# A hybrid attention and RWKV-7 block: each attention step's small matmuls tied into one group, low-rank products issued ahead of both sigmoids, the last chunk's outputs tied together

## The chip, the cores and the metric

One core of one Trainium2 chip runs the whole kernel. The metric is the device time in microseconds (us) of one execution; a run is repeated and its median taken. Lower is better.

## What is computed

One decoder layer on x of 256 x 1024 float32. After an RMS norm, one wide projection feeds two causal token mixers side by side, attention (8 heads of 64, one block of 256, so it is plain causal attention with a linear distance bias) and an RWKV-7 recurrence (8 heads of 64). Each mixer's output is gated by a SiLU path, projected up, multiplied by a sigmoid gate, and the sum goes through one output projection and a second norm.

```
h = rmsnorm(x, norm_pre);  proj = h @ w_in
aq, ak, av, az, rw_stream, rz, g_att, g_rw = split(proj)
ya = attention(aq, ak, av) * silu(az)
rs, ksr, vs, wd, ad = token_shift_mix(rw_stream)
decay = exp(-exp(-softplus(-(w0 + tanh(wd) @ w_up)) - 0.5))     # low-rank product 1
a     = sigmoid(a0 + ad @ a_up)                                 # low-rank product 2
o  = rwkv7_scan(rs, decay, kmod(ksr, a), vs, kk(ksr), a)
yb = (head_groupnorm(o) + bonus) * silu(rz)
u  = sigmoid(g_att) * (ya @ w_up_att) + sigmoid(g_rw) * (yb @ w_up_rw)
out = x + rmsnorm(u @ w_out, norm_post)
```

## The kernel before, in words

**The stream.** All projections run on TensorE in blocks of 512 KB of weights. A block arrives by DMA (tile wraw, issued on SyncE's queue, L117), is split into a rounded high part on ScalarE (whi, L123) and a remainder on VectorE (wlo, L124), and is then used by `proj_tile` (L259) or `up_pair` (L697) through `mm3` (L136): three matmuls of 128 x 128 weights on 256 columns (L137, L138, L139) for each eighth of the block, 24 in all. Splits run up to LOOKAHEAD = 4 blocks ahead. These 24 matmuls a block are the main stream. Their results lie in one of three large PSUM tiles (mmps).

**The lanes.** Everything else on TensorE is small and is let into the stream by hand. Two generators, one for the recurrence (`rw`) and one for attention (`att`), give up control at each `yield`. `pump()` is called three times in a block (after its 3rd, 5th and 8th eighth, L267); each call adds the lane's rate to its credit, and at a credit of 1 the generator runs to its next `yield`. So a rate of 0.32 is one piece of attention for every 3.1 pumps, about one a block. This sets the program's order. A list scheduler then orders each engine's instructions at compile time by that order and by its own model of when operands are ready; a stream matmul that it takes to be unready leaves a hole that a later small matmul may fill. On the chip each engine runs its instructions in the order so fixed, and waits on semaphores.

**Ties.** `one_group` (L334) adds an ordering edge, without a semaphore, from the first matmul of a list to each of the others: none of them can stand ahead of the first. `after` (L329) is that edge; it also keeps sigmoids behind the last softmax (`last_soft`) and exponentials behind the low-rank sigmoids (`last_sig`), for ScalarE's function tables.

**The low-rank products** (`lora_phase`, L339). For each of four head pairs, a small PSUM tile (smps, three of them in all) holds both products. Two matmuls (L347) make the first, a sigmoid on ScalarE (L348) reads it, two more matmuls make the second in the same bank, and a second sigmoid reads that.

**Attention** (`att_phase`, L665) has six steps p = 0 to 5, one for each head pair and two to empty the pipeline. In a step come, each behind a `yield`: the values of pair p - 2 (`att_values`, 4 matmuls written, 8 issued, L658, 128 rows by 64 columns of the array), the transposes of pair p - 1 (`att_transpose`, 6, L651, the full array), and the scores of pair p with its softmax (`att_scores`, 4 written, 8 issued, L628, 64 rows by 128 columns, into the one tile twops). The softmax is VectorE (L635, L637, L642) and ScalarE (L640 to L644); the transposes read it, and ScalarE copies them to pt (L653) for the values, whose result it copies to att_o (L663).

**The recurrence** runs pair phases (`pair_phase`, L372), a triangular inverse of 31 steps on VectorE (`inverse_phase`, L447; L477, L479), then four chunks one after another (`chunks_phase`, L545). In each chunk, L551 makes u, VectorE scales it to UVE and UVO (L554), L561 gives the next state, L523 the next chunk's input, and `chunk_out` (L529; L536 from the state, L538 from UVE and UVO) the output. For chunks 0 to 2 the outputs are tied in one group behind the next chunk's input; the last chunk's outputs stand untied:

```
            if c == NCH - 1:
                chunk_out(c)
```

Each output is then normalised over VectorE and GpSimd (`norm_chunk`, L574) and transposed (L586) for the up-projection of the recurrence, which is the last to use `up_pair`. The output projection (L844) and a short tail on VectorE and the DMA queues end the kernel.

Of the kernel before, what the change touches and what calls it, by code (L numbers as in the profile page):

```python
# [16 lines left out]
P = 128  # L17
T = 256
# [11 lines left out]
WARM = 26  # L30
HP = 100000
HP_FROM = 5
R_ATT, R_SUB, R_CH = 0.32, 0.75, 0.8
NORM_SLOTS = 4
LORA_SLOTS = 4
LOOKAHEAD = 4
# [7 lines left out]
def block_kernel(ctx: ExitStack, tc: tile.TileContext, x, wp, pv, lora, npost, out):  # L44
# [294 lines left out]
    def lora_phase():  # L339
        for _ in range(LORA_SLOTS):  # L340
            yield
        for p in range(NP):
            pl = smps().rearrange("p (n t) -> p n t", n=2)
            fs = slice(p * P, (p + 1) * P)
            for n, (dst, off, lst) in enumerate(((sga, PV_W0, sgs), (aaa, PV_A0, aas))):
                for i in range(2):
                    nc.tensor.matmul(out=pl[:, n], lhsT=lrs[:, n, fs], rhs=wax[:, i, n], start=(i == 0), stop=(i == 1))  # L347
                last_sig.append(nc.scalar.activation(out=dst[:, p, :], in_=pl[:, n], func=AF.Sigmoid, bias=pvc(off, p)))  # L348
                lst.append(dst[:, p, :])
            yield  # L350
# [175 lines left out]
        nc.scalar.copy(out=wsb, in_=w)  # L526
        return wsb, mms

    def chunk_out(c):  # L529


        o = p4(smps())
        mms = []
        for p in range(NP):
            for h, fs, AR, SV, UV, SC in (EV, OD):
                mms.append(mm(out=o[fs, p, :], lhsT=AR[:, p, c, C:2 * C], rhs=SV[:, c, p, :], start=True, stop=False))  # L536
            for h, fs, AR, SV, UV, SC in (EV, OD):
                mms.append(mm(out=o[fs, p, :], lhsT=SC[:, p, c, C:2 * C], rhs=UV[:, c, p, :], start=False, stop=True))  # L538
        o2, osb = p4(tg()), p4(tg())
        nc.scalar.activation(out=o2, in_=o, func=AF.Square)  # L540
        nc.scalar.copy(out=osb, in_=o)
        nm.gens.append(norm_chunk(c, osb, o2))
        return mms

    def chunks_phase():  # L545
# [3 lines left out]
        for c in range(NCH):  # L549
            u = p4(smps())  # L550
            one_group([mm(out=u[fs, p, :], lhsT=X64[fs, p, c, :], rhs=wsb[fs, p, :], start=True, stop=True)  # L551
                       for p in range(NP) for h, fs, AR, SV, UV, SC in (EV, OD)])
            for h, fs, AR, SV, UV, SC in (EV, OD):
                nc.vector.tensor_tensor(out=UV[fs, c], in0=u[fs], in1=rnt[fs, :, c:c + 1].broadcast_to([64, NP, C]), op=ALU.mult)  # L554
            yield
            if c == NCH - 1:
                chunk_out(c)
                yield
                break
            s = p4(smps())  # L560
            one_group([mm(out=s[fs, p, :], lhsT=BKt[:, c, h, p, :], rhs=UV[:, c, p, :], start=True, stop=True)  # L561
                       for p in range(NP) for h, fs, AR, SV, UV, SC in (OD, EV)])
            for h, fs, AR, SV, UV, SC in (EV, OD):
                gc = Gc[fs, :, c, :].broadcast_to([64, NP, C])
                dst = SV[fs, c + 1]
                nc.vector.tensor_tensor(out=dst, in0=s[fs], in1=SV[fs, c], op=ALU.add)
                nc.vector.tensor_tensor(out=dst, in0=dst, in1=gc, op=ALU.mult)
            yield

            wsb, mms = chunk_in(c + 1)  # L570
            one_group(mms + chunk_out(c))
            yield
# [51 lines left out]
    def att_scores(p):  # L624

        qT, kT = qk
        s = twops()
        one_group([nc.tensor.matmul(out=s[:, i, c0:c0 + n], lhsT=qT[LH[i], p, q0:q0 + P], rhs=kT[LH[i], p, 0:n], start=True, stop=True)  # L628
                   for q0, n, c0 in ((0, P, 0), (P, T, P)) for i in (1, 0)])
        for i in range(2):  # L630
            h = 2 * p + i
            lg = tt([P, 384], "lg")
# [12 lines left out]
            lgs[h] = lg  # L645

    def att_transpose(p):
        for h in (2 * p, 2 * p + 1):
            tp = smps()
            for b in range(3):  # L650
                nc.tensor.transpose(out=tp[:, b * P:(b + 1) * P], in_=lgs[h][:, b * P:(b + 1) * P], identity=ident)  # L651
            pts[h] = tt([P, 384], "pt")
            nc.scalar.copy(out=pts[h], in_=tp[:, 0:384])  # L653

    def att_values(p):

        o = smps()
        one_group([nc.tensor.matmul(out=o[LH[i], t0:T], lhsT=vtk[:, b, p * P + i * 64:p * P + i * 64 + 64], rhs=pts[2 * p + i][:, c0:c0 + T - t0],  # L658
                                    start=(b == 0), stop=(b == 1)) for b, t0, c0 in ((0, 0, 0), (1, P, T)) for i in (1, 0)])
        if p == 0:  # L660
            att_all.append(ct([P, NP, T], "gz"))
        att_o[p] = att_all[0][:, p, :]
        nc.scalar.copy(out=att_o[p], in_=o[:, 0:T])  # L663

    def att_phase():  # L665

        for p in range(NP + 2):
            if 2 <= p:
                att_values(p - 2)
            yield  # L670
            if 1 <= p <= NP:
                att_transpose(p - 1)
            yield
            if p < NP:
                att_scores(p)
            yield

    def silu(ps, sg):
# [75 lines left out]
    def main():  # L754
# [16 lines left out]
        for p in range(NP):  # L771
# [5 lines left out]
            with hp():  # L777
                nc.scalar.copy(out=kT[:, p, :], in_=ps)
            if p == 0:
                att.rate = R_ATT  # L780
                att.gens.append(att_phase())
            yield

# [160 lines left out]
```

## Time and profile before

| | |
|---|---|
| median of 3 runs | 256.84 us (256.5 to 257.18) |
| profiled execution, its own time | 255.78 us |
| its span (first to last instruction) | 254.1 us |
| TensorE matmul busy | 240.2 us, 95% of the span |
| VectorE busy | 181.6 us, 71% |
| ScalarE busy | 148.9 us, 59% |
| GpSimd busy | 32.8 us, 13% |
| mean granted TensorE clock | 0.987 of full |

The span is the profiled execution's; what lies around it in its own time of 255.78 us is 1.7 us of start and end. Busy time is the union of an engine's instructions; matmuls overlap, so the distance from the start of one to the start of the next says what it costs in the stream, and its own duration does not. Lines such as L347 are those of the kernel before.

### The profile page before, as it was taken

How to read it: one execution, taken by the hardware profiler on the slowest of the kernel's cores; microseconds unless marked ns; L12 is line 12 of the kernel's file. 1: busy time of each engine (PE TensorE's matmuls, PEld its weight loads, DVE VectorE, ACT ScalarE, POOL GpSimd, SP SyncE). 2: the span in 40 equal slices, each digit the busy share in tenths (PEclk: the TensorE clock that was granted, in tenths of full speed). 3: DMA queues.
4: the chain of work that ended last, by engine and by line, in shares of the span. 5: the costliest groups of instructions: out<-in, count | busy, mean ns of one | idle time of the engine just before them, and what ended most of it. 6: DMA issues, size and time to landing. Idle time of an engine off the chain costs nothing.

```text
span 254.1 us, 5784 instructions
## 1 busy us (share of the span) xinstructions
PE 240.2 (95%) x2283; PEld 220.2 (87%) x2283; DVE 181.6 (71%) x370; ACT 148.9 (59%) x291; POOL 32.8 (13%) x74
## 2 busy tenths in 40 slices
PE   7799699999999999999999999999998999999990
PEld 5599699998788999899898999899896999988890
DVE  2677739999853089999996366987777666998243
ACT  4676799577517277693949765763333543573241
POOL 2735000103015200000004400000112100000000
PEclk9979999999999999999999999999999999999997
DMA  6825955865769958534345576434225766543022
GB/s 232 350 81 152 357 178 181 250 172 134 187 158 216 294 172 277 168 126 144 146 168 146 163 237 201 147 93 161 84 83 181 238 194 215 172 143 106 3 72 94
DMA packets 19500, 43.68 MB, mean 172 GB/s; under 512 B 7536, under 2 KB 8688, under 8 KB 19472
## 3 DMA queue, kind: packets, MB, share of 16 engines
q1 hardware_dynamic: 18336, 41.30, 51.6%
q0 software_dynamic: 704, 1.71, 2.7%
q8 instruction: 18, 0.29, 0.5%
q10 hardware_dynamic: 432, 0.29, 0.4%
q14 instruction: 10, 0.08, 0.1%
HBM read 37.90 MB, written 1.84 MB: 156 GB/s over the span
## 4 chain that ended last, share of the span: by engine, by line
PE 61%; DVE 16%; ACT 8%; DMA 7%; issue 5%; POOL 1%; DVEq 0%; SPq 0%; ACTq 0%; POOLq 0%
PE mmps L137 14%; PE mmps L139 13%; PE mmps L138 13%; PE mmps L844 9%; DVE wlo L124 5%; ACT whi L123 4%; DMA wraw<-in_wp_dram 3%; DVE gen L477 2%; PE mmps L612 2%; DMA BK<-BK 2%; DMA slot<-in_x_dram 2%; DVE slot L479 2%; ACT hh L184 1%; PE smps L347 1%; DVE hl L185 1%
## 5 line engine op out<-in xcount | busy, mean ns | idle before, releaser
L137 PE MATMUL mmps<-hh,whi 128*128 128x256 f32 x336 | 96.7, 288 | 0.0
L138 PE MATMUL mmps<-hl,whi 128*128 128x256 f32 x336 | 94.9, 282 | 0.0
L139 PE MATMUL mmps<-hh,wlo 128*128 128x256 f32 x336 | 94.8, 282 | 0.0
L124 DVE TENSOR_TENSOR wlo<-wraw,whi 128x1024 fp32r<-128x1024 f32 x58 | 71.4, 1234 | 28.2 <-ACT whi L123 27.9
L123 ACT CAST whi<-wraw 128x1024 fp32r<-128x1024 f32 x58 | 60.5, 1048 | 36.8 <-PE mmps L138 21.9
L137 PEld LDWEIGHTS mmps<-hh,whi 128*128 128x128 f32 x336 | 63.3, 188 | 2.7 <-issue 2.0
L139 PEld LDWEIGHTS mmps<-hh,wlo 128*128 128x128 f32 x336 | 63.2, 188 | 0.4
L138 PEld LDWEIGHTS mmps<-hl,whi 128*128 128x128 f32 x336 | 63.3, 188 | 0.3
L477 DVE SCALAR_TENSOR_TENSOR gen<-slot,rnf 64x31 f32<-64x31 f32 (+15 forms) x31 | 12.1, 392 | 0.7
L479 DVE TENSOR_TENSOR slot<-slot,gen 64x31 f32<-64x31 f32 (+15 forms) x31 | 10.3, 333 | 0.7
L580 POOL TENSOR_TENSOR rv<-rv,mhalf 128x4 f32<-128x4 f32 x4 | 4.2, 1049 | 44.7 <-DVE rv L579 44.7
L137 PE MATMUL mmps<-yah,whi 128*128 128x256 f32 x32 | 9.2, 287 | 0.0
L850 DVE TENSOR_TENSOR SCE<-mmps,X 128x512 f32<-128x512 f32 (+1 forms) x5 | 2.9, 583 | 8.7 <-ACT ar L849 8.7
L139 PE MATMUL mmps<-slot,wlo 128*128 128x256 f32 x32 | 9.1, 283 | 0.0
L137 PE MATMUL mmps<-slot,whi 128*128 128x256 f32 x32 | 9.1, 283 | 0.0
L138 PE MATMUL mmps<-slot,whi 128*128 128x256 f32 x32 | 9.1, 283 | 0.0
L138 PE MATMUL mmps<-yal,whi 128*128 128x256 f32 x32 | 9.0, 281 | 0.0
L139 PE MATMUL mmps<-yah,wlo 128*128 128x256 f32 x32 | 9.0, 281 | 0.0
L849 ACT ACTIVATE ar<-mmps 128x512 f32<-128x512 f32 (+1 forms) x5 | 2.6, 513 | 10.7 <-PE mmps L844 10.7
L640 ACT ACTIVATE lg<-lg,mn 128x128 f32<-128x128 f32 x8 | 3.2, 397 | 8.3 <-DVE mn L635 8.3
L191 PE MATMUL mmps<-hl,whi 128*128 128x256 f32 x24 | 7.5, 336 | 0.5 <-DVE hl L185 0.2
L190 PE MATMUL mmps<-hh,whi 128*128 128x256 f32 x24 | 7.6, 339 | 0.2
(260 smaller groups left out, 502.3 us busy)
## 6 DMA issues: line engine op xcount, KB each, us to landing
wraw<-in_wp_dram SPq DMA_DIRECT2D x64, 512.0 KB, 4.2
slot<-in_x_dram SPq DMA_DIRECT2D x2, 512.0 KB, 4.0
wraw<-in_wp_dram SPq DMA_DIRECT2D x2, 256.0 KB, 5.3
gz<-in_lora_dram SPq DMA_DIRECT2D x1, 512.0 KB, 8.1
bonv<-gen SPq DMA_DIRECT2D x8, 64.0 KB, 3.1
ARE<-ar SPq DMA_DIRECT2D x4, 128.0 KB, 3.1
ARO<-ar SPq DMA_DIRECT2D x4, 128.0 KB, 3.1
ARE<-SCE SPq DMA_DIRECT2D x4, 128.0 KB, 2.5
```

Of the source, the lines that this page charges most:

```text
L123: cast = nc.scalar.copy(out=hi[:, a:b], in_=raw[:, a:b])
L124: nc.vector.tensor_tensor(out=lo[:, a:b], in0=raw[:, a:b], in1=hi[:, a:b], op=ALU.subtract)
L137: nc.tensor.matmul(out=o, lhsT=lh, rhs=rh, start=first, stop=False)
L138: nc.tensor.matmul(out=o, lhsT=lh, rhs=rl, start=False, stop=False)
L139: nc.tensor.matmul(out=o, lhsT=ll, rhs=rh, start=False, stop=last)
L190: nc.tensor.matmul(out=started[n][:, 0:T], lhsT=ws, rhs=hh[:, k, :], start=(k == 0), stop=False)
L191: nc.tensor.matmul(out=started[n][:, 0:T], lhsT=ws, rhs=hl[:, k, :], start=False, stop=False)
L477: nc.vector.scalar_tensor_tensor(out=pr, in0=fl[:, s, s + 1:32].unsqueeze(2).broadcast_to([64, n, s + 1]), scalar=rnf[:, s:s + 1], in1=tb[ ...
L479: nc.vector.tensor_tensor(out=tb[:, s + 1:32, 0:s + 1], in0=tb[:, s + 1:32, 0:s + 1], in1=pr, op=ALU.add)
L580: nc.gpsimd.tensor_tensor(out=rv, in0=rv, in1=mhalf, op=ALU.pow)
L612: nc.tensor.matmul(out=pa[i], lhsT=a[:, k, ts], rhs=w[:, wsl], start=(k == 0 and n == 0), stop=(k == KD - 1 and n == 2))
L844: nc.tensor.matmul(out=ps, lhsT=a[:, k, ts], rhs=w[:, wsl], start=(k == 0 and m == 0), stop=(k == KD - 1 and m == 2))
```

## The change

In `lora_phase` all four matmuls of a pair are issued before its two sigmoids. In `att_phase` a step's three pieces are issued at one pump in place of three, in the order values, scores, transposes, and tied to the first matmul among them; the softmax follows. The lane's rate falls to a third (0.32 to 0.107), and it starts with a credit of 0.7, so its steps fall on pumps 3, 13, 22, 31, 41 and 50 after the first key block. Before, the scores fell on pumps 10, 19, 29 and 38, the transposes on 16, 25, 35 and 44, the values on 22, 32, 41 and 50. In `att_transpose` both PSUM tiles are taken and written before either is copied. `chunk_out` for the last chunk is tied in one group and multiplies with UVO and UVE first, then with the state. The diff, cut where lines only move:

```diff
-R_ATT, R_SUB, R_CH = 0.32, 0.75, 0.8
+R_ATT, R_SUB, R_CH = 0.107, 0.75, 0.8
...
 def lora_phase():
...
-            for n, (dst, off, lst) in enumerate(((sga, PV_W0, sgs), (aaa, PV_A0, aas))):
+            for n in range(2):
                 for i in range(2):
                     nc.tensor.matmul(out=pl[:, n], lhsT=lrs[:, n, fs], rhs=wax[:, i, n], start=(i == 0), stop=(i == 1))
+            for n, (dst, off, lst) in enumerate(((sga, PV_W0, sgs), (aaa, PV_A0, aas))):
                 last_sig.append(nc.scalar.activation(out=dst[:, p, :], in_=pl[:, n], func=AF.Sigmoid, bias=pvc(off, p)))
                 lst.append(dst[:, p, :])
...
-    def chunk_out(c):
+    def chunk_out(c, late=True):
...
         for p in range(NP):
-            for h, fs, AR, SV, UV, SC in (EV, OD):
-                mms.append(mm(out=o[fs, p, :], lhsT=AR[:, p, c, C:2 * C], rhs=SV[:, c, p, :], start=True, stop=False))
-            for h, fs, AR, SV, UV, SC in (EV, OD):
-                mms.append(mm(out=o[fs, p, :], lhsT=SC[:, p, c, C:2 * C], rhs=UV[:, c, p, :], start=False, stop=True))
+            for n in range(2):
+                for h, fs, AR, SV, UV, SC in (EV, OD) if late else (OD, EV):
+                    a, b = ((AR, SV), (SC, UV))[n ^ (not late)]
+                    mms.append(mm(out=o[fs, p, :], lhsT=a[:, p, c, C:2 * C], rhs=b[:, c, p, :], start=(n == 0), stop=(n == 1)))
...
             if c == NCH - 1:
-                chunk_out(c)
+                one_group(chunk_out(c, late=False))
...
     def att_scores(p):
...
-        one_group([nc.tensor.matmul(out=s[:, i, c0:c0 + n], ...) ...])
+        return s, [nc.tensor.matmul(out=s[:, i, c0:c0 + n], ...) ...]
+
+    def att_softmax(p, s):
         for i in range(2):
...
     def att_transpose(p):
-        for h in (2 * p, 2 * p + 1):
-            tp = smps()
+        tps, mms = [smps(), smps()], []
+        for i, tp in enumerate(tps):
             for b in range(3):
-                nc.tensor.transpose(out=tp[:, b * P:(b + 1) * P], in_=lgs[h][:, b * P:(b + 1) * P], identity=ident)
-            pts[h] = tt([P, 384], "pt")
-            nc.scalar.copy(out=pts[h], in_=tp[:, 0:384])
+                mms.append(nc.tensor.transpose(out=tp[:, b * P:(b + 1) * P], in_=lgs[2 * p + i][:, b * P:(b + 1) * P], identity=ident))
+        for i, tp in enumerate(tps):
+            pts[2 * p + i] = tt([P, 384], "pt")
+            nc.scalar.copy(out=pts[2 * p + i], in_=tp[:, 0:384])
+        return mms
...
     def att_values(p):
...
-        one_group([nc.tensor.matmul(...) ...])
+        mms = [nc.tensor.matmul(...) ...]
...
+        return mms
...
         for p in range(NP + 2):
+            mms = []
             if 2 <= p:
-                att_values(p - 2)
-            yield
+                mms += att_values(p - 2)
+            if p < NP:
+                s, m = att_scores(p)
+                mms += m
             if 1 <= p <= NP:
-                att_transpose(p - 1)
-            yield
+                mms += att_transpose(p - 1)
+            one_group(mms)
             if p < NP:
-                att_scores(p)
+                att_softmax(p, s)
             yield
...
-                att.rate = R_ATT
+                att.rate, att.credit = R_ATT, 0.7
```

## Rows read from the trace of the kernel before

**Rows 1.** From the profile's page: the busy line of its first part (engine, busy us, share of the span, instructions) and one of its second part, TensorE's granted clock in 40 equal slices (9 is 90% or more of full).

```profile
PE 240.2 (95%) x2283; PEld 220.2 (87%) x2283; DVE 181.6 (71%) x370; ACT 148.9 (59%) x291; POOL 32.8 (13%) x74
...
PEclk9979999999999999999999999999999999999997
```

**Rows 2.** Busy time by stage (windows view): the stretch in us from the span's start, its length, and for PE, PEld, DVE, ACT and POOL the busy us (and instructions); then the granted TensorE clock, the DMA engines' busy share and GB/s. The stretches are the whole middle of the kernel, the pair phases of the recurrence, and attention with most of the inverse.

```profile
22.00:248.00 226.00, 221.19 (x2167) 204.17 (x2165) 166.35 (x338) 135.54 (x268) 20.82 (x36) 1.00 0.55 170
42.00:60.00 18.00, 17.65 (x218) 16.87 (x217) 17.36 (x36) 12.95 (x25) 2.80 (x7) 1.00 0.66 188
...
91.00:131.00 40.00, 40.00 (x328) 36.52 (x327) 38.02 (x98) 28.17 (x67) 0.00 (x0) 1.00 0.52 172
```

**Rows 3.** The waits of TensorE, longest first in total: what waited, for what, us in total, times, longest.

```profile
PE smps L347 <- ACT qT L348: 2.0, 1, 2.0
PE smps L523 <- DVE SVO L567: 1.5, 2, 1.1
...
PE smps L406 <- DVE gen L402: 0.4, 1, 0.4
```

**Rows 4.** TensorE's timeline inside one projection block (start us, us, engine, line, operation, tiles, shapes, count; the first and the last of 22 matmuls in a row).

```profile
130.45 0.28 PE L138 MATMUL mmps<-hl,whi 128*128 128x256 f32 x1
...
133.06 0.28 PE L139 MATMUL mmps<-hh,wlo 128*128 128x256 f32 x1
```

**Rows 5.** TensorE's timeline at the low-rank products of the first pair (L347; brackets give the idle time ahead and what ended it).

```profile
26.09 0.60 PE L347 MATMUL smps<-yal,yah 128*128 128x256 f32 x2
...
27.24 0.28 PE L137 MATMUL mmps<-hh,whi 128*128 128x256 f32 x1
29.51 0.47 PE L347 MATMUL smps<-yal,yah 128*128 128x256 f32 x2 [1.99 <-ACT qT L348]
29.82 0.28 PE L138 MATMUL mmps<-hl,whi 128*128 128x256 f32 x1
```

**Rows 6.** ScalarE's timeline beside it: the first pair's first sigmoid.

```profile
28.89 0.47 ACT L348 ACTIVATE qT<-smps,pvt 128x256 f32<-128x256 f32 x1
```

**Rows 7.** TensorE's timeline around one step's values (L658), one step's transposes (L651) and one step's scores (L628), each between matmuls of the projection stream.

```profile
109.70 0.28 PE L139 MATMUL mmps<-hh,wlo 128*128 128x256 f32 x1
109.91 0.87 PE L658 MATMUL smps<-pt,vtk 128*64 128x256 f32 x8
110.71 0.38 PE L137 MATMUL mmps<-hh,whi 128*128 128x256 f32 x1
110.93 0.28 PE L138 MATMUL mmps<-hl,whi 128*128 128x256 f32 x1
...
113.55 0.28 PE L139 MATMUL mmps<-hh,wlo 128*128 128x256 f32 x1
113.67 0.82 PE L651 MATMUL smps<-ident,lg 128*128 128x128 f32 x6
...
114.44 0.28 PE L138 MATMUL mmps<-hl,whi 128*128 128x256 f32 x1
...
117.77 0.28 PE L139 MATMUL mmps<-hh,wlo 128*128 128x256 f32 x1
117.98 0.93 PE L628 MATMUL twops<-kT,qT 64*128 64x128 f32 x8
118.83 0.39 PE L137 MATMUL mmps<-hh,whi 128*128 128x256 f32 x1
119.06 0.28 PE L138 MATMUL mmps<-hl,whi 128*128 128x256 f32 x1
```

**Rows 8.** TensorE's timeline where a group of the first step's scores (L628) and of the last step's transposes (L651) is broken.

```profile
91.02 0.28 PE L138 MATMUL mmps<-hl,whi 128*128 128x256 f32 x1
91.23 0.48 PE L628 MATMUL twops<-kT,qT 64*128 64x128 f32 x2
...
91.87 0.28 PE L137 MATMUL mmps<-hh,whi 128*128 128x256 f32 x1
...
136.88 0.28 PE L139 MATMUL mmps<-hh,wlo 128*128 128x256 f32 x1
...
137.67 0.84 PE L651 MATMUL smps<-ident,lg 128*128 128x128 f32 x3 [0.19 <-ACT lg L643]
...
138.47 0.28 PE L138 MATMUL mmps<-hl,whi 128*128 128x256 f32 x1
```

**Rows 9.** Timelines of the softmax of the last step: the scores on TensorE, and the last of the four normalisations on ScalarE.

```profile
129.37 0.93 PE L628 MATMUL twops<-kT,qT 64*128 64x128 f32 x8
...
137.51 0.51 ACT L644 ACTIVATE lg<-lg,l 128x256 f32<-128x256 f32 x1
```

**Rows 10.** TensorE's timeline at the outputs of a middle chunk, from the first of 32 matmuls to the group of another shape (L551) behind them, and of the last chunk, whose 32 matmuls stand in three pieces with seven projection matmuls between and behind them up to the last row.

```profile
176.20 0.22 PE L536 MATMUL smps<-SVO,ARO 128*64 128x64 f32 x1
...
177.26 0.68 PE L551 MATMUL smps<-gen,X 64*64 64x64 f32 x16
...
194.25 0.27 PE L536 MATMUL smps<-SVE,ARE 128*64 128x64 f32 x1
...
195.88 0.27 PE L538 MATMUL smps<-UVO,SCO 128*64 128x64 f32 x1
...
197.06 0.28 PE L137 MATMUL mmps<-hh,whi 128*128 128x256 f32 x1
```

**Rows 11.** TensorE's timeline where the up-projection of the recurrence begins (it reads the normalised outputs; their tile is named slot).

```profile
213.66 0.28 PE L137 MATMUL mmps<-slot,whi 128*128 128x256 f32 x1
```

More of the change, by code (lines that the diff above doesn't have):

```diff
@@ L627, in att_scores @@
         s = twops()
-        one_group([nc.tensor.matmul(out=s[:, i, c0:c0 + n], lhsT=qT[LH[i], p, q0:q0 + P], rhs=kT[LH[i], p, 0:n], start=True, stop=True)
-                   for q0, n, c0 in ((0, P, 0), (P, T, P)) for i in (1, 0)])
+        return s, [nc.tensor.matmul(out=s[:, i, c0:c0 + n], lhsT=qT[LH[i], p, q0:q0 + P], rhs=kT[LH[i], p, 0:n], start=True, stop=True)
+                   for q0, n, c0 in ((0, P, 0), (P, T, P)) for i in (1, 0)]
+    def att_softmax(p, s):
         for i in range(2):
@@ L647, in att_transpose @@
     def att_transpose(p):
-        for h in (2 * p, 2 * p + 1):
-            tp = smps()
+        tps, mms = [smps(), smps()], []
+        for i, tp in enumerate(tps):
             for b in range(3):
-                nc.tensor.transpose(out=tp[:, b * P:(b + 1) * P], in_=lgs[h][:, b * P:(b + 1) * P], identity=ident)
-            pts[h] = tt([P, 384], "pt")
-            nc.scalar.copy(out=pts[h], in_=tp[:, 0:384])
+                mms.append(nc.tensor.transpose(out=tp[:, b * P:(b + 1) * P], in_=lgs[2 * p + i][:, b * P:(b + 1) * P], identity=ident))
[3 more added lines that the diff above has]
+        return mms
     def att_values(p):
         o = smps()
-        one_group([nc.tensor.matmul(out=o[LH[i], t0:T], lhsT=vtk[:, b, p * P + i * 64:p * P + i * 64 + 64], rhs=pts[2 * p + i][:, c0:c0 + T - t0],
-                                    start=(b == 0), stop=(b == 1)) for b, t0, c0 in ((0, 0, 0), (1, P, T)) for i in (1, 0)])
+        mms = [nc.tensor.matmul(out=o[LH[i], t0:T], lhsT=vtk[:, b, p * P + i * 64:p * P + i * 64 + 64], rhs=pts[2 * p + i][:, c0:c0 + T - t0],
+                                start=(b == 0), stop=(b == 1)) for b, t0, c0 in ((0, 0, 0), (1, P, T)) for i in (1, 0)]
         if p == 0:
```

## The prediction

> **What bounds the kernel now.** I read the page first, then the windows by stage, TensorE's waits, and last its timeline at single excursions from the stream. TensorE is busy for 95% of the span at full clock nearly throughout [rows 1], and from 22 to 248 us for 221.2 of 226 us [rows 2]. No other engine comes near in that stretch: VectorE has 166.4 us, ScalarE 135.5 us. In attention VectorE is close, 38.0 of 40 us, and in the pair phases 17.4 of 18 us [rows 2]; that is the first thing to fear. The waits confirm the reading: past 22 us TensorE waits long for three causes only, 2.0 us for a low-rank sigmoid, 1.5 us for the state of a chunk, 0.4 us ahead of L406 [rows 3]. So a microsecond taken out of TensorE's sequence before 248 us is a microsecond of the total, unless it reappears as a wait.
>
> Busy time hides what is inside. The price of a matmul is the distance to the next start. In the plain stream 22 matmuls start between 130.45 and 133.06, so (133.06 - 130.45)/22 = 0.119 us each [rows 4]. For an excursion I take the last stream start ahead of it, the second stream start behind it, and subtract two times 0.119 us. That gives values 110.93 - 109.70 - 0.24 = 0.99 us, transposes 114.44 - 113.55 - 0.24 = 0.65 us, scores 119.06 - 117.77 - 0.24 = 1.05 us [rows 7]. Part of that is not work but the change of the array's shape: ahead of values 0.21 us pass in place of 0.12, and behind them the first stream matmul takes 0.22; the same at scores (0.21 and 0.23). Transposes use the full array and start 0.12 us after the stream matmul ahead, with no such loss on entering [rows 7].
>
> **The low-rank products.** The second product of a pair waits for the first sigmoid, since both lie in one PSUM bank. At the first pair TensorE starts its last stream matmul at 27.24, L347 at 29.51 and the next stream matmul at 29.82 [rows 5]: 2.58 us for three matmuls that cost 0.119 each, 2.2 us lost. The sigmoid ran from 28.89 [rows 6]; ScalarE came to it late, and TensorE, which runs in order, held everything behind. With four matmuls ahead of both sigmoids no product waits for a sigmoid of its own pair. Added: nothing; eight sigmoids and sixteen matmuls as before, no DMA. Late next could be the fourth pair: with three small tiles it needs the first pair's tile, free only after both its sigmoids. It is issued three pumps, about one block of 24 x 0.119 = 2.9 us, after the first pair, whose products start at 26.09 [rows 5]. That is 29 us; the first sigmoid ended at 28.89 + 0.47 = 29.36 [rows 6] and the second would follow within 0.5 us if ScalarE puts nothing between. I take the full 2.2 us, with 1.1 us as the low end (half comes back there) and 2.6 us as the high one, if the 0.4 us ahead of L406 [rows 3] goes too because the sigmoids that feed it end earlier.
>
> **Attention, one group a step.** Apart, one step costs 0.99 + 0.65 + 1.05 = 2.69 us. Tied: entry 0.09, values up to the next start 110.71 - 109.91 = 0.80 (which holds the change of shape at its end), scores 118.83 - 117.98 = 0.85 (likewise), transposes 0.65. The trace has no transposes directly behind scores; entering after another shape may cost between nothing and 0.10 us, as much as the stream pays on its return [rows 7]. I take 0.05, the middle. Sum 2.44, so 0.25 us less. Two steps are like that. Step 1 (scores, transposes) saves 1.05 + 0.65 - (0.09 + 0.85 + 0.05 + 0.65) = 0.06, step 4 (values, transposes) 0.05, steps 0 and 5 nothing. Together 0.6 us. The small size is the point: the group still changes shape twice inside.
>
> The Trainium skill says the same against this part: on its page TensorEngine Tiling (Array Packing), under Key Properties, changing the tiling mode, not just the tile, drains the engine. By that rule a step pays three drains in place of four, and merging gives back one of four; without it the two inner changes would be free too, and the saving would be about 0.2 us a step larger. The trace agrees with it: the price stands at every entry and return of the narrow shapes in the row group above and at none of the transposes.
>
> More comes from repairs. The first step's scores are broken: two matmuls stand alone between stream matmuls, at 91.87 - 91.02 - 0.24 = 0.61 us [rows 8]. Their later start was a hole in the order; now the scores come seven pumps earlier, after one whole block, and I expect them whole: 0.6 us. The last step's transposes cost 138.47 - 136.88 - 0.24 = 1.35 us in place of 0.65, with a wait for ScalarE's normalisation [rows 8]: 0.7 us. That wait ends because the transposes move away from their softmax. Now 9.35 pumps, or 9.35/3 x 2.86 = 8.9 us of stream, and the next group's values and scores (0.09 + 0.80 + 0.85) lie between, 10.6 us from the end of the scores; the last softmax took from 130.3 (129.37 + 0.93) to 138.0 (137.51 + 0.51), 7.7 us [rows 9]. The copies that ScalarE now does ahead of the softmax, two of pt and one of att_o, have 2.9 us of cover. If that cover is gone, the wait of 0.7 us comes back. Attention: 0.6 + 0.6 + 0.7 = 1.9 us; low end 0.6, high end 2.4 with the inner changes free.
>
> VectorE and ScalarE do the same work. The first softmax moves ahead of 91 us. No DMA issue moves on any queue, SyncE's and GpSimd's included, except as their data come earlier.
>
> **The last chunk.** A middle chunk's 32 outputs run from 176.20 to 177.26, 1.06 us with the change of shape at their end [rows 10]. The last chunk's lie in three pieces from 194.25 to 197.06, with seven stream matmuls: 2.81 - 7 x 0.119 = 1.98 us [rows 10]. Tied: 0.09 entry + 1.06 + 0.10 return = 1.25, so 0.7 us less. Price: the group can't start before UVO and UVE are both ready, where the outputs from the state alone started at 194.25; stream matmuls fill that, and the norm of this chunk ends later by under 2 us. Its reader begins at 213.66 [rows 11], 16 us later, so this delay is covered. Ends: 0 (TensorE waits for UVO) to 0.8 us.
>
> **Sum.** 2.2 + 1.9 + 0.7 = 4.8 us. The profiled execution's 255.78 us become 251.0; its span 254.1 becomes 249.3. The median of the runs shown is 1.06 us above that execution, so the forecast for a median is 256.84 - 4.8 = 252.0 us. Ends: 1.1 + 0.6 + 0 = 1.7 us (255.1) and 2.6 + 2.4 + 0.8 = 5.8 us (251.0); a new order at compile time can also move waits such as the chunks' 1.5 us [rows 3] either way, up to 249.5 if they all went.
>
> **Rivals.** First, *the waits come back elsewhere or the ties don't hold*: the fourth pair waits for a PSUM tile, and a group's first matmul is pulled into a hole with the rest far behind, as the first scores were, at 0.6 us each. For it: both happen in this trace [rows 5, 8]. Against: the other scores and values shown here are whole [rows 7]. With a gain of 1.1 on the low-rank part, 0.6 in attention, 0.7 at the chunk: 2.4 us, 254.4 us.
>
> Second, *VectorE becomes the bound in attention*: 38.0 of 40 us leave 2.0 us [rows 2]. If splits then came late, TensorE could not shorten that stretch by its full 1.9 us; losing most of it gives 253.6 us. Against: the inverse in that load has no reader before the chunks, so it can slip while splits keep their turn.
>
> Third, on the other side, *transposes tied to their group arrive before their softmax*. TensorE runs in order, so a late normalisation on ScalarE would stop the whole stream, four times. It decides at a softmax of more than 10.6 us in place of 7.7. To lose the 4.8 us, four waits of over 1.2 us are needed, a softmax of 11.8 us; at 12.5 us it costs 4 x 1.9 = 7.6, giving 256.84 - 4.8 + 7.6 = 259.6 us. For it: three evacuations now stand together on ScalarE. Against: the 2.9 us of cover.
>
> Fourth, *nothing changes*: what TensorE saves is lost in front of the chunks, whose chain of TensorE, VectorE and ScalarE already waits 1.5 us [rows 3]. Then 256.8 us.
>
> **How the numbers follow.** Forecast 0.74, first rival 0.12, second 0.07, third 0.04, fourth 0.03. The first two are faster too, so faster by over 0.3% (0.8 us, about what a measurement of this kernel can tell from none) has 0.93, within it 0.03, slower 0.04. The range of 249.9 to 254.7 us holds the forecast with its ends and nearly all of the first two rivals.
>
> **What would show it.** Right: no idle time ahead of L347's successor; one excursion a step in attention, six in all, the full ones near 2.44 us; the first scores and last transposes whole; the last chunk's outputs in one piece of about 1.1 us; stream matmuls still 0.119 us apart; TensorE's stream ending near 243 us in place of 248. Wrong: an idle TensorE at transposes or ahead of the last chunk's group, scores alone in the stream, or a wait for wlo in attention. If the sum is wrong while each part is right, the lost time is in the chunks.

## The result, and the profile after

The changed kernel takes 255.23 us (median of 7 runs, 253.3 to 256.5) where the kernel before takes 257.18 us beside it (7 runs, 256.5 to 259.07): a ratio of 0.990, 95% interval 0.9863 to 0.9937. It is faster, by about 2.6 us by that ratio (1.95 us by the medians), where 4.8 us were forecast, and 255.23 us lies above the forecast's range, which ends at 254.7. Measured again on another chip it gave 0.9856 (0.9824 to 0.9887), 3.7 us less.

The profiled execution of the kernel after is one of those runs, 255.23 us, with a span of 253.5 us. Its line numbers shift: from L348 on by one, from L628 on by one to five, in the output projection by more. Its page, first the busy line, then the granted TensorE clock (compare [rows 1]):

```profile
PE 238.7 (94%) x2283; PEld 220.8 (87%) x2283; DVE 181.2 (72%) x370; ACT 149.4 (59%) x291; POOL 32.8 (13%) x74
...
PEclk9979999799999999999999999999999999999998
```

The eighth digit of the clock is new: around 46 to 50 us the clock was halved for a while. TensorE's waits, longest first (total us, times, longest; compare [rows 3]):

```profile
PE mmps L137 <- DVE k L274: 2.2, 1, 2.2
PE smps L524 <- DVE SVO L568: 1.5, 2, 1.1
...
PE smps L587 <- DVE gen L582: 1.1, 1, 1.1
...
PE smps L407 <- DVE gen L403: 0.2, 1, 0.2
```

The wait of L347 is gone, 2.0 us. At the top stand two that the kernel before did not have: a stream matmul that waits 2.2 us for the shift of a key tile, and the transposes at L587 that wait 1.1 us for a normalised chunk. The forecast has neither of these two.

To see where the microseconds lie, cut the span at three events of TensorE's timeline: the first stream matmul of L137 (at 21.51 us before, 21.77 after), the inverse's first product (L500 before, L501 after) and the first matmul of the output projection. Before, the stretches are 137.86 and 65.81 us; after, 136.95 and 65.87 us. The last chunk lies in the second stretch, which did not shrink at all. The first holds the low-rank products and attention; it shrank by 0.9 us.

**Attention did what was forecast.** TensorE's timeline around one full step and the stream matmuls on either side (start us, us, engine, line, operation, tiles, shapes, count):

```profile
110.75 0.28 PE L139 MATMUL mmps<-hh,wlo 128*128 128x256 f32 x1
110.95 0.87 PE L663 MATMUL smps<-pt,vtk 128*64 128x256 f32 x8
111.76 0.93 PE L629 MATMUL twops<-kT,qT 64*128 64x128 f32 x8
112.61 0.87 PE L654 MATMUL smps<-ident,lg 128*128 128x128 f32 x6
113.24 0.36 PE L137 MATMUL mmps<-hh,whi 128*128 128x256 f32 x1
113.45 0.28 PE L138 MATMUL mmps<-hl,whi 128*128 128x256 f32 x1
```

By the prediction's own measure the step costs 113.45 - 110.75 - 0.24 = 2.46 us; forecast 2.44. There are six such excursions, none broken, none with a wait. Measured in the same way they add up to 1.05 + 1.66 + 2.46 + 2.46 + 1.60 + 0.99 = 10.2 us, where the pieces before added up to 12.6 us: 2.3 us less, forecast 1.9.

**The low-rank products ran as forecast, and the gain was given back.** The first pair's four matmuls now stand together and nothing waits:

```profile
26.34 0.63 PE L347 MATMUL smps<-yal,yah 128*128 128x256 f32 x4
26.81 0.28 PE L137 MATMUL mmps<-hh,whi 128*128 128x256 f32 x1
```

Some 16 us later TensorE stops at the start of a block. It is the eighth of L137 and the eleventh of all; the text below calls it the tenth, counted from zero, as the expectations do (brackets: idle time ahead, and what ended it):

```profile
43.25 0.28 PE L139 MATMUL mmps<-hh,wlo 128*128 128x256 f32 x1
45.76 0.38 PE L137 MATMUL mmps<-hh,whi 128*128 128x256 f32 x1 [2.23 <-DVE k L274]
...
47.80 0.41 PE L139 MATMUL mmps<-hh,wlo 128*128 128x256 f32 x1
48.01 0.41 PE L137 MATMUL mmps<-hh,whi 128*128 128x256 f32 x1
```

The block needs one of the three large PSUM tiles. The oldest still holds the key projection of the third block back, which the shift reads: first ScalarE (L273), then VectorE (L274). ScalarE's timeline ahead of it:

```profile
32.04 1.28 ACT L384 ACT_TABLE_LOAD   x1
33.33 0.42 ACT L384 ACTIVATE gen<-gen 128x256 f32<-128x256 f32 x1
33.77 1.28 ACT L349 ACT_TABLE_LOAD   x1
...
39.26 1.28 ACT L381 ACT_TABLE_LOAD   x1
...
42.72 1.03 ACT L123 CAST whi<-wraw 128x1024 fp32r<-128x1024 f32 x1
43.66 0.47 ACT L273 ACTIVATE k<-mmps,omu 128x256 f32<-128x256 f32 x1
```

and VectorE's behind it:

```profile
44.10 1.22 DVE L124 TENSOR_TENSOR wlo<-wraw,whi 128x1024 fp32r<-128x1024 f32 x1
45.23 0.47 DVE L274 SCALAR_TENSOR_TENSOR k<-mmps,pvt,k 128x255 f32<-128x255 f32 x1
```

Before, the same shift ran on ScalarE at

```profile
41.51 0.48 ACT L273 ACTIVATE k<-mmps,omu 128x256 f32<-128x256 f32 x1
```

and TensorE came to the block at

```profile
46.63 0.28 PE L137 MATMUL mmps<-hh,whi 128*128 128x256 f32 x1
```

so nothing waited. Now TensorE is there at 43.25 + 0.12 = 43.37, 3.3 us sooner, and the shift comes 2.15 us later, because ScalarE did one more split cast and a table load with its exponential first. Of the 3.3 us, 0.9 is left (46.63 - 45.76), and about 0.5 of that is work that moved: the matmuls of L406 stood ahead of the block before and stand behind it now. Could ScalarE have been sooner? In this order it had no idle time to give. The windows (length, then busy us and instructions of PE, PEld, DVE, ACT and POOL, clock, DMA share, GB/s), before:

```profile
31.00:42.00 11.00, 11.00 (x90) 10.64 (x89) 6.50 (x11) 10.94 (x18) 0.00 (x0) 1.00 0.55 189
42.00:46.00 4.00, 4.00 (x34) 3.96 (x33) 3.97 (x9) 3.98 (x8) 0.63 (x3) 1.00 0.74 243
```

After:

```profile
31.00:42.00 11.00, 11.00 (x96) 11.00 (x96) 5.63 (x9) 10.93 (x18) 0.38 (x1) 1.00 0.61 197
42.00:46.00 4.00, 1.77 (x16) 1.57 (x15) 4.00 (x8) 3.06 (x5) 0.11 (x1) 1.00 0.59 206
```

ScalarE was busy for 14.92 of these 15 us before the change. TensorE was the bound of the whole middle, and in this part ScalarE was as full; a faster TensorE came to wait. VectorE has a share in the length of the halt, since its split of 1.22 us at 44.10 stands between the two halves of the shift. But such a split stands there before the change too (41.65, with the shift at 42.80), so it is not what moved.

**The last chunk** is in one piece, and the time is lost at once behind it:

```profile
194.56 0.27 PE L539 MATMUL smps<-UVO,SCO 128*64 128x64 f32 x1
...
195.49 0.22 PE L539 MATMUL smps<-SVE,ARE 128*64 128x64 f32 x1
196.78 0.41 PE L587 MATMUL smps<-ident,gen 128*128 128x128 f32 x2 [1.07 <-DVE gen L582]
```

The next instruction in TensorE's order is the transposes of chunk 2's output, whose normalisation goes through VectorE, GpSimd and VectorE:

```profile
194.74 0.16 DVE L580 TENSOR_SCALAR rv<-rv 128x4 f32<-128x4 f32 x1
...
196.21 0.43 DVE L582 TENSOR_TENSOR gen<-gen,rv 128x256 f32<-128x256 f32 x1 [0.93 <-POOL rv L581]
```

```profile
195.05 1.12 POOL L581 TENSOR_TENSOR rv<-rv,mhalf 128x4 f32<-128x4 f32 x1 [0.49 <-DVE rv L580]
```

Of that chain, the first sum was formed ahead of UVE and UVO on VectorE, and the row of 194.74 comes behind them. Before, the broken outputs and their stream matmuls [rows 10] filled the same time, and the transposes came at

```profile
197.43 0.41 PE L586 MATMUL smps<-ident,gen 128*128 128x128 f32 x2
```

just as the chain was done (its last product ended at 197.28). The outputs were slow, and cost nothing.

### The profile page after: what moved, and what is told of

The parts are those of the page before. It is cut to its first block, busy times and chain, and to the rows that moved or that the text cites. A ratio compares the mean times of both kernels' runs of the same rounds, so it can differ in the third digit from the quotient of the medians.

```text
span 253.5 us, 5779 instructions
## 1 busy us (share of the span) xinstructions
PE 238.7 (94%) x2283; PEld 220.8 (87%) x2283; DVE 181.2 (72%) x370; ACT 149.4 (59%) x291; POOL 32.8 (13%) x74
## 4 chain that ended last, share of the span: by engine, by line
PE 78%; DVE 8%; ACT 5%; issue 4%; DMA 2%; POOL 1%; DVEq 0%; SPq 0%; ACTq 0%; POOLq 0%
PE mmps L137 17%; PE mmps L138 16%; PE mmps L139 16%; PE mmps L853 9%; PE mmps L613 3%; DVE wlo L124 2%; ACT whi L123 2%; DMA slot<-in_x_dram 2%; PE mmps L191 1%; PE twops L629 1%; PE smps L654 1%; POOL rv L581 1%; PE smps L663 1%; PE mmps L190 1%; PE twops L422 1%
## 5 line engine op out<-in xcount | busy, mean ns | idle before, releaser
L137 PE MATMUL mmps<-hh,whi 128*128 128x256 f32 x336 | 96.6, 288 | 2.2 <-DVE k L274 2.2
L137 PEld LDWEIGHTS mmps<-hh,whi 128*128 128x128 f32 x336 | 63.9, 190 | 3.5 <-DVE k L274 2.4
L138 PEld LDWEIGHTS mmps<-hl,whi 128*128 128x128 f32 x336 | 63.9, 190 | 0.3
L137 PE MATMUL mmps<-yah,whi 128*128 128x256 f32 x32 | 9.2, 287 | 0.0
L137 PE MATMUL mmps<-slot,whi 128*128 128x256 f32 x32 | 9.1, 283 | 0.0
L858 ACT ACTIVATE ar<-mmps 128x512 f32<-128x512 f32 (+1 forms) x5 | 2.6, 514 | 10.2 <-PE mmps L853 10.2
L191 PEld LDWEIGHTS mmps<-hl,whi 128*128 128x128 f32 x24 | 5.5, 229 | 1.4 <-DVE hl L185 1.4
```

What stands on the lines that cost most here:

```text
L137: nc.tensor.matmul(out=o, lhsT=lh, rhs=rh, start=first, stop=False)
L138: nc.tensor.matmul(out=o, lhsT=lh, rhs=rl, start=False, stop=False)
L191: nc.tensor.matmul(out=started[n][:, 0:T], lhsT=ws, rhs=hl[:, k, :], start=False, stop=False)
```

## Experiments

**Each part alone.** The kernel before with one part of the change each: the four matmuls of a pair ahead of its sigmoids, or all that concerns attention, or the last chunk's tie and order.

```diff
 # lora_alone: lora_phase alone
-            for n, (dst, off, lst) in enumerate(...):
+            for n in range(2):
                 for i in range(2):
                     nc.tensor.matmul(out=pl[:, n], ...)
+            for n, (dst, off, lst) in enumerate(...):
 # att_alone: R_ATT, the credit, att_scores/softmax/transpose/values/phase alone
 # chunk_alone: chunk_out alone
-                chunk_out(c)
+                one_group(chunk_out(c, late=False))
```

> The kernel before with the low-rank edit alone. The prediction's sum says 2.2 us less (254.6 beside a 256.8). Theory S (ScalarE runs without a break from about 27 to 45 us, so what TensorE gains at 27 us it gives back about 16 us later, when a block needs a large PSUM tile that ScalarE and VectorE have not emptied): the 2.0 us wait for the low-rank sigmoid is gone, a wait of 1.5 to 2.5 us stands ahead of a stream matmul between 40 and 48 us, and the time is within 0.5 us of before, or up to 2 us above it where the granted clock halves behind that wait. Rival V (the wait in the changed kernel comes from the attention edit's other order, not from this one): no such wait, 2 us less.

Measured: 0.9953 (0.9916 to 0.9989), 1.2 us less, more than Theory S allowed and half of what the sum says. The wait of L347 is gone and the new one stands in its place, larger:

```profile
PE mmps L137 <- DVE k L274: 2.6, 1, 2.6
```

So it is the low-rank edit, and nothing else, that brings the wait at the tenth block. Against the profile before, the first stretch is 0.5 us shorter (137.35 us), and not in front of attention: with the order shifted, the first step's scores happened to stay whole and the last transposes cost 1.00 in place of 1.35 us; attention's excursions add up to 11.7 us in place of 12.6. At the place where it was made, the edit gained nothing by these rows: 80 stream matmuls behind the values' projection, ahead of all attention, TensorE stands 67.9 us from its first stream matmul, and 67.5 us before. The granted clock was full there, so the wait takes the gain back without any loss of clock.

> The kernel before with the attention edit alone (one pump a step, its rate and credit). The sum says 1.9 us less, from 0.6 for shape changes, 0.6 for the unbroken first scores, 0.7 for the wait at the last transposes. From the changed kernel's profile, whose six groups are whole and free of waits, I expect 2.2 to 2.8 us less. A rival, that the gain needs the low-rank edit (different starting times), expects under 1 us. The 2.0 us wait for the low-rank sigmoid stays.

Measured: 0.9874 (0.9831 to 0.9917), 3.2 us. Six whole groups, 10.2 us in all, as in the changed kernel; L347 waits as before:

```profile
PE smps L347 <- ACT qT L348: 2.2, 1, 2.2
```

By these estimates attention alone is worth as much as the whole change.

> The kernel before with the last chunk's edit alone. The sum says 0.7 us less. Theory N (TensorE's next instructions behind the group are the transposes of the chunk before, and these wait for GpSimd's power and VectorE's product behind it, which no edit moves): the outputs take 1.1 us in one piece, the transposes then wait 0.8 to 1.3 us, and the time is within 0.3 us of before.

Measured: 0.9995 (0.9965 to 1.0024), with 1.1 us of waiting at the transposes of chunk 2's output (L586 there) and 65.84 us from the inverse's first product to the output projection. The interval of the ratio alone would leave room for the 0.7 us; the stretch, 65.81 us before, does not. The part is worth nothing.

**The change without its low-rank part.**

```diff
 # no_lora: after the change, lora_phase as before
-            for n in range(2):
-                for i in range(2):
-                    nc.tensor.matmul(out=pl[:, n], ...)
             for n, (dst, off, lst) in enumerate(...):
+                for i in range(2):
+                    nc.tensor.matmul(out=pl[:, n], ...)
```

> The changed kernel without the low-rank edit (attention and last chunk alone). Theory S (the low-rank gain is given back at the tenth block, sometimes with a halved clock on top): the 2.0 to 2.3 us wait for the low-rank sigmoid is back, none stands ahead of the tenth block, and the time is that of the changed kernel or up to 1.5 us less: ratio 0.984 to 0.990. The prediction's sum expects 2.2 us more than the changed kernel, 0.998.

Measured: 0.9887 (0.9861 to 0.9912). The changed kernel, run again beside it:

> The changed kernel once more, to stand beside the others of this set on one chip. Its ratio to before was 0.990; expected 0.985 to 0.993. If the wait of 2.2 us ahead of the tenth block is a property of the order, it stands in this profile too, whether or not the granted clock halves behind it in this execution.

Measured: 0.9856 (0.9824 to 0.9887). By the estimates the low-rank part is worth 0.3% (0.8 us) beside the attention part, and by the overlapping intervals that is not clear of nothing; the 2.2 us forecast would be 0.9%. The two profiles, one execution each, show no gain: from the first stream matmul to the inverse's first product it takes 135.70 us without the part and 135.88 us with it. The wait at the tenth block stood again (2.1 us), but the clock behind it did not halve; more on that below.

**ScalarE relieved.** In the changed kernel an exponential of the pair phase (L384) falls between low-rank sigmoids, as it did before, which makes ScalarE change its function tables three times, 1.28 us each. Here it is held behind them, so that one load is left:

```diff
-        nc.scalar.activation(out=gi, in_=cs, func=AF.Exp, scale=DECAY_SCALE)
+        after(nc.scalar.activation(out=gi, in_=cs, func=AF.Exp, scale=DECAY_SCALE), last_sig)
```

> The changed kernel with one more ordering edge: each pair's second exponential stands behind the last low-rank sigmoid, as the first one does already, so that ScalarE loads its function table once between 27 and 45 us in place of three times (two loads of 1.28 us less). Theory S (ScalarE sets the time there): the wait of 2.2 us ahead of the tenth block goes down to under 0.5 us, the granted clock stays full there, and the time is 2 to 4 us below the changed kernel, 251 to 253 us. Rival V (VectorE's queue holds the evacuation): the wait stays above 1.1 us and the gain is under 1 us. Rival C (the loss is the halved clock, whatever brings it): the half clock stays and so does the time.

Measured: 0.9863 (0.9817 to 0.9908). The key shift comes at 39.97 in place of 43.66, and its half on VectorE ends at 42.10, ahead of the 43.37 at which TensorE came to the block in the changed kernel. The wait at the tenth block is gone; that ScalarE's load caused it is shown. The two loads saved are 2 x 1.28 = 2.6 of the 43.66 - 39.97 = 3.7 us. The Trainium skill (ScalarE: Activation LUTs, What ACT_TABLE_LOAD costs) puts a switch at 2.66 us, half of it a drain; the trace does not agree, since the instruction behind the load of 32.04 starts at 33.33, 1.29 us on, and the load itself starts where the sigmoid ahead of it ends (31.54 + 0.48). But the time is about that of the changed kernel and not 2 to 4 us below it, since the waits moved to the next stations of the pair phase:

```profile
PE smps L407 <- DVE gen L403: 1.6, 2, 1.2
PE twops L422 <- DMA BK<-BK: 1.6, 1, 1.6
```

TensorE is now ahead of VectorE's chain to L407, and of the small transfer of BK behind it. With two more yields ahead of L407, so that the pair phase asks for it later:

```diff
         yield
+        yield
+        yield
         mm = nc.tensor.matmul
         pb = smps()
```

> The kernel with the second exponential tied behind the sigmoids, and with two pumps more in each pair phase ahead of its matmuls (L407, L422). In the kernel with the tie alone, the wait ahead of the tenth block is gone, but 1.6 us at L407 and 1.6 us at L422 came in its place. Theory P (TensorE has caught up with the pair phases' chain over ScalarE, VectorE and DMA, and any 2 us gained ahead of it are given back unless its matmuls stand later in the order): both waits fall below 0.5 us together, and the time falls by 1.5 to 3 us against the kernel with the tie alone, 251 to 252 us beside a 257.4. Rival D (the chain as a whole, not its place in the order, is too slow, and VectorE with it): the waits move on to the next reader, the inverse or a weight block, and the time stays within 0.5 us.

Measured: 0.9828 (0.9795 to 0.9861); these two waits fall from 3.2 to 1.2 and 0.4 us, not both below 0.5. In the profile the first stretch is 133.64 us, 2.2 us less than in the second profile of the changed kernel. In the times that is not shown: the median is 253.89 us beside 253.84 us for the changed kernel on the same chip, and the intervals overlap. Nor does a run have these two edits without the low-rank part, so what is gained here need not be the low-rank gain.

**The last chunk's transposes put off.** Six pieces of waiting between a chunk's normalisation and its transposes in place of four:

```diff
-NORM_SLOTS = 4
+NORM_SLOTS = 6
```

> The changed kernel with the transposes of each normalised chunk let in two pumps later (six in place of four). Theory N: the wait of 1.1 us at the transposes behind the last chunk's group goes, since GpSimd's power and VectorE's product are then done, and the time falls by 0.7 to 1.2 us against the changed kernel. Rival: the last chunk's group itself waits, or the wait moves to the up-projection that reads the norm; then no gain.

Measured: 0.9844 (0.9818 to 0.987). No wait at L587, and 64.60 us in place of 65.87 us from the inverse's first product to the output projection: what the transposes held up was 1.3 us. The ratio to before is 0.3 us lower than that of the changed kernel on the same chip, less than the 0.7 to 1.2 us expected, and the intervals overlap, so the times do not show it. Whether the tie of the last chunk's outputs gains anything here stays open: no run has the later transposes without the tie.

**Attention's steps closer together.** The prediction put the end of the wait at the last transposes down to the distance from the softmax. Here the distance is cut to what the softmax took before:

```diff
-R_ATT, R_SUB, R_CH = 0.107, 0.75, 0.8
+R_ATT, R_SUB, R_CH = 0.16, 0.75, 0.8
```

> The changed kernel with attention's rate at 0.16 in place of 0.107: a step comes every 6.25 pumps in place of 9.35, so 50 stream matmuls (6.0 us) in place of 75 (8.9 us) lie between two groups, and 7.7 us in place of 10.6 us from the end of a step's scores to the next group's transposes. Theory that this distance is what took the wait out of the transposes (the last step's softmax took 7.7 us before, and two copies on ScalarE now stand ahead of it): TensorE idles ahead of the transposes for a normalisation on ScalarE, 0.2 to 1.5 us at each of the four groups that hold them, 1 to 5 us in all, and the time is 0.4 to 2% above that of the changed kernel. Rival, that the waits at transposes went for another reason (the softmax became shorter, since nothing of the stream's work stands between its pieces): no wait at the transposes, and the time within 0.3% of the changed kernel's.

Measured: 0.9903 (0.9866 to 0.994), the changed kernel's first ratio (0.5% above its second), and no wait at any transposes. It is the missing wait that makes the theory fall. The last step's values and transposes, whole:

```profile
120.35 0.87 PE L663 MATMUL smps<-pt,vtk 128*64 128x256 f32 x8
121.15 0.88 PE L654 MATMUL smps<-ident,lg 128*128 128x128 f32 x6
121.78 0.37 PE L137 MATMUL mmps<-hh,whi 128*128 128x256 f32 x1
```

The last normalisation on ScalarE ended at 120.13, only 6.1 us behind its scores (113.06 + 0.93):

```profile
119.63 0.50 ACT L647 ACTIVATE lg<-lg,l 128x256 f32<-128x256 f32 x1
```

In the changed kernel it took 8.5 us, before 7.7 us. This softmax had no duration of its own: it took what the order of VectorE and ScalarE left it. Before, the last reciprocal on VectorE stood behind a split and the inverse's closing copy:

```profile
136.38 0.15 DVE L642 RECIPROCAL l<-l 128x2 f32<-128x2 f32 x1
```

But ScalarE came to the normalisation that reads it later still, and without idle time, since a split cast and a copy stood ahead of it in ScalarE's order:

```profile
136.00 1.05 ACT L123 CAST whi<-wraw 128x1024 fp32r<-128x1024 f32 x1
136.95 0.36 ACT L788 COPY BK<-mmps 128x256 f32<-128x256 f32 x1
137.21 0.41 ACT L643 ACTIVATE lg<-lg,l 128x128 f32<-128x128 f32 x1
```

**All repairs together**: the exponential held back, the two yields and NORM_SLOTS = 6. (NORM_SLOTS counts pieces of waiting, as above; where the expectation calls them small buffers it is wrong.)

> The changed kernel with three additions that were run apart before: the exponential of the pair phases placed behind the low-rank sigmoids and two more pieces of waiting in the pair phase (0.983 together), and six small buffers for the normalised outputs in place of four (which took 1.2 us out of the time between the inverse's first product and the output projection). Theory that the places are independent of each other (each is one wait in another stage): no wait at the tenth block, none for chunk 2's normalisation at the last chunk's transposes, 64.6 us in place of 65.8 us from the inverse's first product to the output projection, 1.0 to 1.3 us less than with the first two additions alone: a ratio of 0.978 to 0.980 to the kernel before. Rival, that a wait which goes comes back at the next chunk or in the pair phases: ratio 0.983 or more and 65.8 us still.

Measured: 0.9817 (0.9773 to 0.9862), 252.29 us. From the inverse's first product to the output projection it takes 64.60 us, as expected; at L407's place (L409 there) 1.8 us of waiting remain. The places are not independent, as the theory had it: the ratio misses its 0.978 to 0.980 and lies only 0.3 us below that of the first two additions alone (measured on another chip). In this profile the first stretch is 135.89 us in place of 133.64; the granted clock halved behind those 1.8 us (see the end), which is one part of it. By the intervals it is faster than the kernel before, and its estimate is below the changed kernel's 0.990 and 0.9856, though its interval overlaps that of the second measurement.

## Why the prediction was wrong

**Attention: right in mechanism and nearly in size.** 2.3 us against 1.9. The terms, by the same measure: a full step 2.46 us (forecast 2.44), the first scores 0.6 us, the last values and transposes 2.34 to 1.60, 0.7 us, all as forecast. Inside a group the changes of shape cost what the returns to the stream did: the next kind starts 0.81 us behind the start of the values and 0.85 us behind that of the scores, the stream before 0.80 and 0.85 [rows 7]. The extra comes from two more sets of transposes, not shown in [rows 8]: before, the first ones lay in three pieces and cost 0.92 in place of 0.65 us, and the third, in one piece, cost 0.83. The prediction looked at the last set only. One reason was wrong though the number held: the wait at the last transposes did not end because of the distance. The step "the last softmax took ... 7.7 us" treated as a property what was one order of VectorE and ScalarE, and the rival built on it, a softmax later than its transposes, was priced from the same number. The middle value of 0.05 us for entering transposes from scores was about right: behind the scores the second stream matmul starts 113.45 - 112.61 = 0.84 us after the first transpose, behind the stream it did so 114.44 - 113.67 = 0.77 us after it [rows 7]. One reading of the rows was half right, that the price of the shape "stands ... at none of the transposes". On entering it is so. But behind them the first stream matmul takes 114.44 - 114.24 = 0.20 us too, though the shape does not change there:

```profile
114.24 0.36 PE L137 MATMUL mmps<-hh,whi 128*128 128x256 f32 x1
```

So that the 0.10 us on return come from the change of shape is not shown; the 0.09 us on entering fit it.

**The low-rank products: the step that failed.** "I take the full 2.2 us, with 1.1 us as the low end". By the rows it is net about nothing: 2.0 us of waiting went at L347, and 2.2 us came at the tenth block. By the times it is 0.8 us (0.9887 to 0.9856), not clear of nothing. The prediction did ask what is late next, and looked no further than the fourth pair's small PSUM tile, 3 us on. That one was in time: the fourth pair's matmuls run at 30.57. What was late next lay 16 us on and on another resource, a large PSUM tile whose reader is ScalarE. The sign of it was in the trace before: the prediction read ScalarE over the whole middle, 135.5 of 226 us [rows 2], where 31 to 46 us alone shows 14.92 of 15. It had written that "a microsecond taken out of TensorE's sequence" is one of the total "unless it reappears as a wait", and it did not take a window of the other engines just behind the place where TensorE gets ahead. The first rival said that waits come back; it named the wrong place and kept half of the gain. That its 2.4 us lies near the 2.6 measured is luck: of its parts (1.1, 0.6 and 0.7 us) none came so.

**The last chunk: 0.7 us forecast, none measured.** The failed step is "stream matmuls fill that, and the norm of this chunk ends later by under 2 us. Its reader begins at 213.66 [rows 11], 16 us later". It followed the last chunk's norm and not that of chunk 2, whose transposes are TensorE's very next instruction, at L587. The order before had spread the outputs over just the time that this norm needs, so tidying them turned filled time into idle time.

**The sum.** 2.3 + 0 + 0 = 2.3 us, against about 2.6 us by the ratio (3.7 us in the second measurement). The profiles fit the 2.3 us: the first stretch is 0.9 us shorter where the clock halved, which cost some 1.5 us (below), and 2.0 us shorter in the second profile (135.88 us), where it did not. What the ratios have beyond that, up to 1.4 us, no row places. With all the repairs the kernel takes 252.29 us, near the forecast of 252.0 us; but that is no support for the sum, since the repairs also take away two table loads that the forecast did not count, and leave waits of 1.8 and 0.7 us in the pair phases.

## What to carry to other kernels

Where the change makes the bounding engine faster at one place, take a window of the other engines just behind that place: one that is full there, however idle it is over the whole, can take the gain back. Ahead of tidying a broken group, look at what the next instruction of that engine waits for; untidy work that fills a wait is free. And don't carry the latency of a chain over from one order to another: the same softmax took 6.1, 7.7 and 8.5 us in three orders of the same engines.

## What was not expected of the hardware

In the profiled execution the halt at the tenth block had a second price: behind 2.23 us of idle time, and a few matmuls after it, TensorE's granted clock fell to half for 3.4 us. The same stretch in the changed kernel as first profiled, and then in its second profile, where the halt was 2.1 us and the clock did not fall:

```profile
46.67:50.08 3.41, 3.41 (x16) 3.23 (x16) 2.56 (x5) 0.67 (x2) 0.00 (x0) 0.50 1.01 244
```

```profile
46.67:50.08 3.41, 3.41 (x28) 3.36 (x29) 3.32 (x7) 0.94 (x3) 0.00 (x0) 1.00 0.88 255
```

At half the clock a stream matmul takes 48.01 - 47.80 = 0.21 us where it takes 0.119 at full clock [rows 4]. From the matmuls of L407 to the thirtieth stream matmul behind them 52.02 - 46.57 = 5.45 us passed, and 51.23 - 47.33 = 3.90 us in the second profile: about 1.5 us lost.

The clock fell in the same way in three more profiles: behind a halt of 2.1 us (attention's steps closer together; granted 0.50 of full from 48 to 50 us), of 2.0 us (the transposes put off; 0.56 from 48 to 50 us) and of 1.8 us (all repairs; 0.61 from 44.96 to 48 us). In the profile of the low-rank edit alone it stayed full (1.00 from 46.1 to 50 us) behind the longest halt of all at this place, 2.6 us. It stayed full, too, behind the halts of 2.0 to 2.3 us at L347 in the four profiles that have them (1.00 from 29.4 to 36 us). So the length of the halt alone does not decide it.

The changed kernel's 13 executions in the two measurements fall in two groups: seven of 253.3 to 254.07 us with a mean granted clock of 0.988 or more, and six of 255.23 to 256.5 us at 0.986 or less. That this halt makes the groups is not shown: the kernel before has none at this place, and in 22 executions beside the parts it spreads from 255.6 to 259.26 us at 0.975 to 0.997. With the exponential held back, where the longest halt is 1.6 us, all six lie between 253.3 and 254.08 us, but with the two yields as well, where it is 1.2 us, they spread from 252.01 to 254.42 us. Why the clock falls in some executions and not in others, behind the same halt, stays open. So does one question of the code: whether the common pump or the tie made attention's groups whole. No run has one without the other.
